# Feed-forward opening: normed tokens of the second half kept in fp32 by the norm, in place of sums of their two fp16 halves

## The chip, the cores and the metric

The kernel runs on one core of a Trainium2 chip. The metric is the device time of one execution in microseconds. The core has a matrix engine (TensorE, PE in the profile), three engines for elementwise work (VectorE is DVE, ScalarE is ACT, GpSimd is POOL) and DMA queues that are started here by SyncE (SP). Each engine works through its own instructions in order; semaphores hold an instruction until others have ended.

## The reference

Two layers of a transformer for 1024 latent and 256 context tokens of width 1024, everything in fp32. A layer is

```python
h  = rms_norm(x, norm_mix) * (1 + sc1) + sh1     # sc, sh, g: from the conditioning c
q, k, v, mlstm, gates, pool = split(h @ w_in)
x  = x + g1 * (concat(attention, mlstm, pool_mix) @ w_out)
h2 = rms_norm(x, norm_ffn) * (1 + sc2) + sh2
x  = x + g2 * ((silu(h2 @ w_gate) * (h2 @ w_up)) @ w_down)     # width 2816
```

The change lies between `h2` and the first products of the feed-forward. In the second layer the context tokens have no feed-forward.

## The kernel before

**Precision.** A product in fp32 is made of fp16 products: a value is split into a high half (its rounding to fp16) and a low half (the rest), and three matmuls (high by high, high by low, low by high) are summed. The usual split is one instruction of ScalarE for the high half and one of VectorE for the low half. Everything on chip lies as 128 partitions by columns; a token tile `h2[:, k, half, tokens]` holds feature block k of eight, its high or low half, and the tokens as columns. `h2` lies in the large tile T1 (`T_72` in the orders below), the queries, keys and values of the attention, and later the activations, in a second one, T2 (`T_73`). Rows of the profile call both `T`.

**The feed-forward** multiplies by blocks with seven products in place of eight, as Strassen did: the tokens are halved into H0 (0 to 511) and H1 (512 to 1023), the features into blocks 0 to 3 and 4 to 7. Three of the seven products need transformed tokens: with r11 = features 0-3 of H0, r12 = features 0-3 of H1 and r22 = features 4-7 of H1, T1 = r12 - r11, T3 = r22 - r12, T2 = r22 - T1. A fourth, T4, is (features 4-7 of H0) - T2. T1 to T3 are kept as split halves in tiles called `tq`; T4 is formed in fp32 in a part of T2 (`scv`) and written over H1 of `h2` when the plain H1 is no longer read. The weights are halved and summed in the same manner: their sums (`ws`) are made by GpSimd from raw tiles (`st`, `raw`) that SyncE fetches, and their split pieces (`hlp`) by ScalarE (high) and VectorE (low). Pieces are A11 to A22 and S1 to S4. The products (L1960) go to the banks Swa, Swb and Swc, a tile of weights with 512 tokens at a time; the sums and what follows are taken from the banks by VectorE.

**The norm** (`norm_k`, L595) makes `h2` from the residual X, for one feature block and some tokens: VectorE scales (`t<-X,prm,sq`, in fp32), ScalarE adds the shift and rounds (`T<-t,prm`, high half), VectorE makes the low half (`T<-t,prm,T`). Where the flag `mix` is set (blocks 2 and 5) ScalarE writes the shifted fp32 value back to `t`, then the high half, and GpSimd makes the low half. The tokens of H1 are normed in two parts of 256 columns: 512 to 767 while the output projection of the last part is still running (`wod`, splits of its weights `hlr`), and 768 to 1023 after it.

**The opening** (up to L1796) is the stretch between the norm and the seven-product steps. Ahead of it two strips of 128 gate and up features are multiplied plainly: `Sg`, `Su`, from which ScalarE makes Silu (`sg<-Sg`) and VectorE the gate product (`sg<-Su,sg`). While this runs, `h_ops` (L1544) is stepped four times, once per feature block k. A step rebuilds fp32 tokens as the sum of their halves (`rb<-T`, three), subtracts (`rb<-rb`, three), splits T3, T2 and T1 (three on ScalarE, three on VectorE: `tq<-rb,tq`) and updates T4 (`T<-T,rb`): ten instructions of VectorE. From the first gate product on VectorE keeps the order in which the program is written (`in_row(True)`); the other engines are ordered by a scheduler. The steps stand in that order by `next(ho)`: one ahead of the second `sg`, one behind it, in layer 0 one ahead of the last `sg` (768 columns), the rest behind the first weight pieces (`prepare()`).

**Buffers.** `t`, `rb`, `ws` and the squares share one ring of six buffers of 128x512 fp32, so each new tile waits until the one six places ahead of it has had its last reader. The raw weights have two `st` buffers, and the transfer into one is queued when its last reader is through. ScalarE also carries out the table loads ahead of a change of function.

Of the kernel before, what the change touches and what calls it, by code (L numbers as in the profile page):

```python
# [18 lines left out]
P = 128  # L19
# [62 lines left out]
def hybrid_kernel(ctx: ExitStack, tc: tile.TileContext, I, out, dbg=None):  # L82
# [89 lines left out]
    def act(o, i, f=AF.Copy, **kw):  # L172
        if f in (AF.Exp, AF.Ln) and tabs["kind"] != "el":
            preload()
        b = S.activation(o, i, f, **kw).ins  # L175
        if tabs.get("copy") is not None:
            tc.add_manual_dep(b, tabs["copy"].name, order, reason="behind the last copy")
        if f in (AF.Exp, AF.Ln):
            after(b, tabs["pre"])
            tabs["last"] = tabs["last"][-7:] + [b]  # L180
        elif f in (AF.Tanh, AF.Silu):
            if tabs["kind"] != f:
                for j in tabs["last"]:
                    after(b, j)
                tabs.update(last=[], kind=f)
            for j in tabs["last"][-1:]:
                after(b, j)
            tabs["last"] = [b]
        return b
# [397 lines left out]
    def rms_spread(s, ms, rr):  # L587
# [4 lines left out]
        act(r[:, :s.n], ms[:, :s.n])  # L592
        return r

    def norm_k(l, q, h, t0, n, k, r, pool=False, mix=False):  # L595
        s = 1 if t0 >= T else 0
        t = f2k((P, 512), F32, "t")
        stt(t[:, :n], X[:, k, t0:t0 + n], prm[l][:, q + 1, k, s:s + 1], r[:, :n], MUL, MUL)
        if pool:
            G.tensor_scalar(t[:, :n], t[:, :n], prm[l][:, q, k, s:s + 1], 1.0, op0=ADD, op1=MUL)  # L600
            act(h[:, k, 0, t0:t0 + n], t[:, :n])
            tt(h[:, k, 1, t0:t0 + n], t[:, :n], h[:, k, 0, t0:t0 + n], SUB, G)
            return
        if mix:
            act(t[:, :n], t[:, :n], AF.Identity, bias=prm[l][:, q, k, s:s + 1])
            act(h[:, k, 0, t0:t0 + n], t[:, :n])
            tt(h[:, k, 1, t0:t0 + n], t[:, :n], h[:, k, 0, t0:t0 + n], SUB, G)
            return
        act(h[:, k, 0, t0:t0 + n], t[:, :n], AF.Identity, bias=prm[l][:, q, k, s:s + 1])
        stt(h[:, k, 1, t0:t0 + n], t[:, :n], prm[l][:, q, k, s:s + 1], h[:, k, 0, t0:t0 + n], ADD, SUB)  # L610

    def norm(l, q, h, t0, n, sums, wait=1):
        for _ in range(wait):
# [153 lines left out]
    for l in range(DEPTH):  # L767
# [776 lines left out]
        def h_ops():  # L1544

            sl = [pt_((P, 2, 2, 512), F16, "phl", PHB, "tq") for _ in range(PHB)]
            sl += [pt_((P, 2, 2, 512), F16, "pT", PTB, "tq") for _ in range(6 - PHB)]
            pcs = [s[:, i] for s in sl for i in range(2)]
            for z, op in enumerate(("T1", "T2", "T3")):
                tpc[op] = pcs[4 * z:4 * z + 4]  # L1550
            for k in range(4):
                r12, r11, r22 = (f2k((P, 512), F32, "rb") for _ in range(3))
                for r, kk, c in ((r22, 4 + k, H1), (r12, k, H1), (r11, k, H0)):
                    tt(r, h2[:, kk, 0, c], h2[:, kk, 1, c], ADD)
                tt(r11, r12, r11, SUB)
                tt(r12, r22, r12, SUB)
                tt(r22, r22, r11, SUB)
                for op, r in (("T3", r12), ("T2", r22), ("T1", r11)):
                    split2(tpc[op][k], r, V)
                tt(scv[:, k], scv[:, k], r22, SUB)  # L1560
                yield
# [220 lines left out]
                fm(S_[:, t0:t0 + n], w, h2, t0, n)  # L1782
        wt = w = S_ = None
        act(sg[:, 512:NTq], Sg[:, 512:NTq], AF.Silu, scale=INV)
        if not last:
            next(ho)
        stt(sg[:, 512:NTq], Su[:, 512:NTq], 1.0 / SW, sg[:, 512:NTq], MUL, MUL)
        del Sg, Su
        hlt += [wk.tile([P, 2048], F16, tag="hl", name="hlp", bufs=2) for _ in range(2)]
# [278 lines left out]
```

## Time and profile before

| | |
|---|---|
| median of 3 runs | 2776.61 us (2774.57, 2776.61, 2776.82) |
| the profiled execution | 2780.47 us, its span 2778.7 us |
| instructions | 53623 |
| TensorE busy | 2564.7 us, 92% of the span, 21403 matmuls |
| VectorE busy | 1890.2 us, 68%, 3233 instructions |
| ScalarE busy | 1387.1 us, 50%, 2650 instructions |
| GpSimd busy | 1269.3 us, 46%, 963 instructions |
| granted TensorE clock, mean | 0.969 of 2.4 GHz |

The shares are means over the whole span, in which TensorE is the busiest by far. The change lies in two stretches of some 50 us, one in each layer (about 725 to 775 and 2145 to 2196 us), and in the norms ahead of them. What bounds the kernel there is read from the busy time of each engine in these stretches and from what TensorE waits for in them, not from the table.

### The profile page before, as it was taken

What the parts mean: (1) busy time and instruction counts of PE and PEld (TensorE: products, weight loads), DVE (VectorE), ACT (ScalarE), POOL (GpSimd) and SP (SyncE); (2) the same over time, 40 slices, a digit from 0 to 9 for tenths busy, and PEclk for the clock granted to TensorE, in tenths of its full rate; (3) what the DMA queues carried; (4) which work ended last, traced back from release to release, by engine and by line L of the source; (5) the groups of instructions that cost most, each with busy time, mean ns of one, the idle gap of its engine ahead of it and who ended that gap; (6) DMA issues with size and microseconds to landing.
All of it is one profiled execution on the core that took longest, in us unless ns stands there. A gap on an engine that the chain in (4) does not pass through costs nothing. (4 is left out here: it accounts for less than half of the span.)

```text
span 2778.7 us, 53623 instructions
## 1 busy us (share of the span) xinstructions
PE 2564.7 (92%) x21403; PEld 1500.9 (54%) x21403; DVE 1890.2 (68%) x3233; ACT 1387.1 (50%) x2650; POOL 1269.3 (46%) x963
## 2 busy tenths in 40 slices
PE   7999989987899999999999998888878899999997
PEld 4875556655555555555554684455545344444444
DVE  5558867778766555656565557866777767667676
ACT  5345557766443434444344544466765444444453
POOL 1124446774334435444443213456763465555651
PEclk9999999999899999999999999999989899999999
DMA  9544489995132222223212222389993111111211
GB/s 301 144 123 113 126 203 184 190 177 121 57 92 81 87 84 84 86 82 92 61 46 78 69 55 57 115 185 182 191 174 102 46 53 54 62 61 54 61 53 76
DMA packets 631629, 296.21 MB, mean 107 GB/s; under 512 B 362888, under 2 KB 620756, under 8 KB 630868
## 3 DMA queue, kind: packets, MB, share of 16 engines
q1 hardware_dynamic: 631204, 292.73, 42.9%
q8 instruction: 167, 2.74, 0.4%
q14 instruction: 82, 0.67, 0.1%
q10 hardware_dynamic: 176, 0.07, 0.0%
HBM read 176.19 MB, written 20.87 MB: 71 GB/s over the span
## 5 line engine op out<-in xcount | busy, mean ns | idle before, releaser
L1960 PEld LDWEIGHTS <-hlp 128*128 128x128 f16 x5040 | 492.0, 98 | 602.7 <-issue 26.6
L1960 PE MATMUL Swb<-T,hlp 128*128 128x512 f16 x1920 | 445.6, 381 | 18.5 <-DVE sg L96 13.0
L195 POOL TENSOR_TENSOR phl<-pf,phl 128x1280 f16<-128x1280 f32 (+1 forms) x132 | 345.2, 2618 | 176.8 <-ACT phl L175 123.1
L96 DVE SCALAR_TENSOR_TENSOR hlp<-ws,hlp 128x512 f16<-128x512 f32 (+1 forms) x320 | 231.6, 732 | 112.0 <-ACT hlp L175 89.2
L175 ACT ACTIVATE hlp<-ws 128x512 f16<-128x512 f32 (+1 forms) x320 | 162.6, 518 | 210.7 <-PE Swb L1960 90.5
L175 ACT ACTIVATE pf<-Sp,mx,rq 128x1280 f32<-128x1280 f32 (+1 forms) x144 | 189.6, 1317 | 118.1 <-DVE mx L96 98.8
L96 DVE TENSOR_REDUCE mx<-Sp 128x1 f32<-128x1280 f32 (+1 forms) x132 | 195.0, 1477 | 63.4 <-PE Sp L1337 55.4
L1960 PE MATMUL Swb<-tq,hlp 128*128 128x512 f16 x960 | 223.4, 382 | 8.0 <-DVE hlp L96 4.6
L1960 PE MATMUL Swc<-T,hlp 128*128 128x512 f16 x960 | 227.2, 379 | 0.0
L1400 PE MATMUL pwo<-T,hl 128*128 128x512 f16 (+1 forms) x960 | 194.5, 354 | 34.0 <-DVE X L96 14.3
L492 PE MATMUL pfm<-T,hl 128*128 128x512 f16 (+1 forms) x1032 | 216.4, 363 | 4.2 <-ACT E L175 4.1
L1337 PE MATMUL Sp<-T 128*128 128x512 f16 (+1 forms) x800 | 169.3, 348 | 42.5 <-ACT pf L175 40.1
L96 DVE SCALAR_TENSOR_TENSOR hlp<-st,hlp 128x256 f16<-128x256 f32 (+1 forms) x201 | 149.0, 746 | 86.7 <-ACT hlp L175 73.8
L195 POOL TENSOR_TENSOR ws<-st 128x256 f32<-128x256 f32 (+1 forms) x97 | 104.4, 1083 | 170.1 <-DMA st<-in_w_ffn_down_dram 67.9
L175 ACT ACTIVATE T<-sg 128x512 f16<-128x512 f32 (+1 forms) x170 | 98.8, 599 | 165.0 <-POOL sg L195 96.3
L1972 PE MATMUL dx<-T,hlp 128*128 128x256 f16 x1440 | 177.3, 273 | 1.0 <-DVE hlp L96 1.0
L195 POOL TENSOR_TENSOR X<-X,T 128x512 f32<-128x512 f32 x80 | 114.1, 1427 | 139.8 <-DVE X L96 105.1
L1960 PE MATMUL Swa<-T,hlp 128*128 128x512 f16 x720 | 169.3, 380 | 0.0
L1972 PEld LDWEIGHTS <-hlp 128*128 128x128 f16 x1440 | 139.1, 100 | 33.1 <-issue 4.8
L1400 PEld LDWEIGHTS <-hl 128*128 128x128 f16 x960 | 97.7, 102 | 109.8 <-issue 40.8
L175 ACT ACTIVATE phl<-pf 128x1280 f16<-128x1280 f32 (+1 forms) x115 | 144.6, 1262 | 21.2 <-DMA pT<-phl 18.9
L195 POOL TENSOR_TENSOR sg<-sg,T 128x512 f32<-128x512 f32 x60 | 88.7, 1478 | 143.6 <-DVE T L96 143.2
(308 smaller groups left out, 4735.8 us busy)
## 6 DMA issues: line engine op xcount, KB each, us to landing
T<-in_w_ada_dram SPq DMA_DIRECT2D x48, 512.0 KB
rawa<-in_w_ada_dram SPq DMA_DIRECT2D x48, 512.0 KB
st<-in_w_in_dram SPq DMA_DIRECT2D x32, 512.0 KB
st<-in_w_out_dram SPq DMA_DIRECT2D x64, 256.0 KB
st<-in_w_ffn_gate_dram SPq DMA_DIRECT2D x32, 512.0 KB
st<-in_w_ffn_up_dram SPq DMA_DIRECT2D x30, 512.0 KB
st<-in_w_ffn_down_dram SPq DMA_DIRECT2D x30, 512.0 KB
xs<-X SPq DMA_DIRECT2D x4, 2048.0 KB
```

Source lines behind the costliest of these rows:

```text
L96: b = f(*a, **k)
L175: b = S.activation(o, i, f, **kw).ins
L195: (e or V).tensor_tensor(o, a, b, op=op)
L492: mm(o, w[:, a, k, :], h[:, k, b, t0:t0 + n], start=(k == 0 and j == 0), stop=(k == nk - 1 and j == 2))
L1337: mm(Sp[:, e * nk + b0:e * nk + b0 + m], ql, qkv[:, 4 + h // 4, a, k0 + b0:k0 + b0 + m], start=(a == 0), stop=(a == 1), skip_group_check=True)
L1400: mm(pb, w[:, a, k, :], mixT[:, k0 + k, b, t0:t0 + n], start=(k == 0 and j == 0), stop=(k == 3 and j == 2))
L1960: mm(o, w[:, a, k, :], B[:, b], start=(s in "172" and k == 0 and j == 0), stop=(k == kh(i) - 1 and j == 2), skip_group_check=True)
L1972: mm(dbank[i][:, r * 256:(r + 1) * 256], w[:, a, k, :], B[:, b], start=(first and k == 0 and j == 0), stop=(not first and k == kh(i) - 1 a ...
```

## The change

The norm of the tokens 512 to 1023 ahead of the feed-forward also keeps its result in fp32. The place is a view `kept(k)` of T2, where the queries of the attention stood. For six of the eight feature blocks this is one more instruction of ScalarE, a copy of 128x256 with the shift added, behind the low half; for the two `mix` blocks the value is written there in place of `t`, with no further instruction. `h_ops` uses `kept(k)` and `kept(4 + k)` as r12 and r22, in place: two of its three adds go, and two of its three tiles of the ring. Over two layers and two norms each these are 24 copies, and 16 adds removed. Last, the step of `h_ops` ahead of the last `sg` in layer 0 goes; it is then made with the rest behind the weight pieces.

```diff
--- before.py
+++ after.py
@@ -592,6 +592,11 @@
         act(r[:, :s.n], ms[:, :s.n])
         return r
 
+    def kept(k):
+
+        j = 2 * (k % 4) + k // 4
+        return T2[:, j // 2, j % 2, 0:1024].bitcast(F32)
+
     def norm_k(l, q, h, t0, n, k, r, pool=False, mix=False):
         s = 1 if t0 >= T else 0
         t = f2k((P, 512), F32, "t")
@@ -601,13 +606,17 @@
             act(h[:, k, 0, t0:t0 + n], t[:, :n])
             tt(h[:, k, 1, t0:t0 + n], t[:, :n], h[:, k, 0, t0:t0 + n], SUB, G)
             return
+        keep = kept(k)[:, t0 - 512:t0 - 512 + n] if q and 512 <= t0 < T else None
         if mix:
-            act(t[:, :n], t[:, :n], AF.Identity, bias=prm[l][:, q, k, s:s + 1])
-            act(h[:, k, 0, t0:t0 + n], t[:, :n])
-            tt(h[:, k, 1, t0:t0 + n], t[:, :n], h[:, k, 0, t0:t0 + n], SUB, G)
+            v = t[:, :n] if keep is None else keep
+            act(v, t[:, :n], AF.Identity, bias=prm[l][:, q, k, s:s + 1])
+            act(h[:, k, 0, t0:t0 + n], v)
+            tt(h[:, k, 1, t0:t0 + n], v, h[:, k, 0, t0:t0 + n], SUB, G)
             return
         act(h[:, k, 0, t0:t0 + n], t[:, :n], AF.Identity, bias=prm[l][:, q, k, s:s + 1])
         stt(h[:, k, 1, t0:t0 + n], t[:, :n], prm[l][:, q, k, s:s + 1], h[:, k, 0, t0:t0 + n], ADD, SUB)
+        if keep is not None:
+            act(keep, t[:, :n], AF.Identity, bias=prm[l][:, q, k, s:s + 1])
 
     def norm(l, q, h, t0, n, sums, wait=1):
         for _ in range(wait):
@@ -1549,9 +1558,8 @@
             for z, op in enumerate(("T1", "T2", "T3")):
                 tpc[op] = pcs[4 * z:4 * z + 4]
             for k in range(4):
-                r12, r11, r22 = (f2k((P, 512), F32, "rb") for _ in range(3))
-                for r, kk, c in ((r22, 4 + k, H1), (r12, k, H1), (r11, k, H0)):
-                    tt(r, h2[:, kk, 0, c], h2[:, kk, 1, c], ADD)
+                r12, r22, r11 = kept(k), kept(4 + k), f2k((P, 512), F32, "rb")
+                tt(r11, h2[:, k, 0, H0], h2[:, k, 1, H0], ADD)
                 tt(r11, r12, r11, SUB)
                 tt(r12, r22, r12, SUB)
                 tt(r22, r22, r11, SUB)
@@ -1782,8 +1790,6 @@
                 fm(S_[:, t0:t0 + n], w, h2, t0, n)
         wt = w = S_ = None
         act(sg[:, 512:NTq], Sg[:, 512:NTq], AF.Silu, scale=INV)
-        if not last:
-            next(ho)
         stt(sg[:, 512:NTq], Su[:, 512:NTq], 1.0 / SW, sg[:, 512:NTq], MUL, MUL)
         del Sg, Su
         hlt += [wk.tile([P, 2048], F16, tag="hl", name="hlp", bufs=2) for _ in range(2)]
```

The first place is VectorE in the opening of layer 0, the rows up to the last gate product (`sg`, 768 columns). Before:

```order
L96 TENSOR_TENSOR tq<-rb,tq 128x512 [waits Activation_49] x2
L96 TENSOR_TENSOR tq<-rb,tq 128x512
L96 TENSOR_TENSOR T_73<-T_73,rb 128x512
L96 TENSOR_TENSOR rb<-T_72 128x512 x3
L96 TENSOR_TENSOR T_72<-T_73,T_72 128x512 [waits Activation_49]
L96 TENSOR_TENSOR rb<-rb 128x512 [waits DVE_49]
L96 TENSOR_TENSOR T_72<-T_73,T_72 128x512 [waits Activation_49]
L96 TENSOR_TENSOR rb<-rb 128x512 [waits DVE_49] x2
L96 TENSOR_TENSOR tq<-rb,tq 128x512 [waits Activation_49] x2
L96 TENSOR_TENSOR tq<-rb,tq 128x512
L96 TENSOR_TENSOR T_73<-T_73,rb 128x512
L96 SCALAR_TENSOR_TENSOR sg<-Su,sg 128x768 [waits PE_49]
```

And with the change, from the second gate product on:

```order
L96 SCALAR_TENSOR_TENSOR sg<-Su_10590,sg 128x512 [waits PE_49]
L96 TENSOR_TENSOR rb<-T_72 128x512
L96 TENSOR_TENSOR sg<-sg 128x512 [waits Pool_49]
L96 TENSOR_TENSOR rb<-T_73,rb 128x512 [waits DVE_49]
L96 TENSOR_TENSOR T_73<-T_73 128x512 [waits DVE_49]
L96 TENSOR_TENSOR T_73<-T_73,rb 128x512 [waits DVE_49]
L96 TENSOR_TENSOR tq<-T_73,tq 128x512 [waits Activation_49] x2
L96 TENSOR_TENSOR tq<-rb,tq 128x512
L96 TENSOR_TENSOR T_73<-T_73 128x512
L96 TENSOR_TENSOR T_73<-sg,T_73 128x512 [waits DVE_49,Activation_49]
L96 TENSOR_TENSOR T_72<-T_73,T_72 128x512 [waits Activation_49] x2
L96 SCALAR_TENSOR_TENSOR sg<-Su,sg 128x768 [waits PE_49]
```

The three sums `rb<-T_72` of a step became one, the differences are written into T_73 itself, and the last `sg` stands ten instructions further ahead, behind the second step and not the third.

The second place is ScalarE at the end of the norm of tokens 768 to 1023 in layer 0, up to the first Silu. Before:

```order
L175 ACTIVATE T_72<-t,prm_141 128x256 [waits DVE_49] x2
L175 ACTIVATE t<-t,prm_141 128x256 [waits DVE_49]
L175 ACTIVATE T_72<-t 128x256 [waits Activation_49]
L175 ACTIVATE T_72<-t,prm_141 128x256 [waits DVE_49] x2
L175 ACT_TABLE_LOAD
L175 ACTIVATE sg<-Sg 128x1280 [waits PE_49]
```

And with the change:

```order
L175 ACTIVATE T_72<-T_73 128x256 [waits Activation_49]
L175 ACTIVATE T_73<-t,prm_141 128x256
L175 ACTIVATE T_72<-t,prm_141 128x256 [waits DVE_49]
L175 ACTIVATE T_73<-t,prm_141 128x256
L175 ACTIVATE T_73<-t,prm_141 128x256 [waits DVE_49]
L175 ACTIVATE T_72<-t,prm_141 128x256 [waits DVE_49]
L175 ACTIVATE T_72<-T_73 128x256 [waits Activation_49]
L175 ACTIVATE T_73<-t,prm_141 128x256
L175 ACTIVATE T_72<-t,prm_141 128x256 [waits DVE_49]
L175 ACTIVATE T_73<-t,prm_141 128x256
L175 ACT_TABLE_LOAD
L175 ACTIVATE sg<-Sg 128x1280 [waits PE_49]
```

Between the high halves (`T_72<-t,prm`) now stand the copies (`T_73<-t,prm`), two of them directly ahead of a row that VectorE releases, one ahead of the table load for the Silu.

The third place is GpSimd in the opening of layer 1: the sums of weights (`ws`) of the first pieces. Before:

```order
L195 TENSOR_TENSOR ws<-st 128x512 [waits DMAHW5_49,Pool_49]
L195 TENSOR_TENSOR T_73<-sg,T_73 128x512 [waits Activation_49]
L195 TENSOR_TENSOR ws<-ws,st 128x512 [waits DVE_49,Activation_49,Pool_49]
L195 TENSOR_TENSOR ws<-st,ws 128x512 [waits DVE_49,Activation_49,Pool_49]
L195 TENSOR_TENSOR ws<-raw 128x512 [waits DMAHW6_49,DVE_49,Pool_49]
```

And with the change:

```order
L195 TENSOR_TENSOR ws<-st 128x512 [waits DMAHW5_49]
L195 TENSOR_TENSOR T_73<-sg,T_73 128x512 [waits Activation_49] x2
L195 TENSOR_TENSOR ws<-ws,st 128x512 [waits Pool_49]
L195 TENSOR_TENSOR ws<-st,ws 128x512 [waits PE_49,Pool_49]
L195 TENSOR_TENSOR ws<-raw 128x512 [waits DMAHW6_49,DVE_49]
```

The order of the sums is the same, but where a sum waited for VectorE and ScalarE to be through with a buffer of the ring it now waits for TensorE or for nothing of theirs.

## Rows read from the trace of the kernel before

**Rows 1.** Busy time by stretch, layers 0 and 1; columns in row one.

```profile
core 0: us, PE busy (x) PEld busy (x) DVE busy (x) ACT busy (x) POOL busy (x), PEclk, DMA share, GB/s
724.80:773.28 48.48, 38.55 (x221) 20.49 (x219) 46.46 (x61) 21.46 (x39) 14.80 (x10) 0.89 0.11 33
2145.40:2195.60 50.20, 38.34 (x149) 15.40 (x147) 45.59 (x61) 20.77 (x37) 17.01 (x11) 0.83 0.07 22
747.40:756.40 9.00, 0.03 (x1) 0.00 (x0) 8.93 (x13) 3.15 (x5) 1.91 (x2) 0.63 0.20 58
756.40:773.28 16.88, 15.92 (x91) 8.03 (x91) 16.88 (x25) 8.58 (x17) 4.36 (x3) 0.89 0.11 32
...
2167.70:2195.70 28.00, 20.01 (x64) 7.25 (x64) 24.07 (x34) 10.93 (x20) 10.81 (x7) 0.72 0.06 20
```

**Rows 2.** TensorE waits, 700-800, 2100-2230 us: total us, times, longest.

```profile
PE Swb L1960 <- DVE sg L96: 9.0, 1, 9.0
...
PE Swb L1960 <- DVE hlp L96: 4.6, 1, 4.6
...
PE Swb L1960 <- DVE sg L96: 4.0, 1, 4.0
PE Swb L1960 <- ACT hlp L175: 3.2, 2, 2.5
```

**Rows 3.** Timeline, VectorE, layer 0: start, us, instruction, [idle before].

```profile
724.81 1.49 DVE L96 SCALAR_TENSOR_TENSOR sg<-Su,sg 128x1280 f32<-128x1280 f32 x1 [2.06 <-ACT sg L175]
726.22 1.89 DVE L96 TENSOR_TENSOR rb<-T 128x512 f32<-128x512 f16 x3
729.78 0.69 DVE L96 TENSOR_TENSOR sg<-sg 128x512 f32<-128x512 f32 x1 [1.68 <-POOL T L195]
...
744.73 4.03 DVE L96 TENSOR_TENSOR rb<-T 128x512 f32<-128x512 f16 x3
...
755.47 0.94 DVE L96 SCALAR_TENSOR_TENSOR sg<-Su,sg 128x768 f32<-128x768 f32 x1
...
772.69 0.68 DVE L96 SCALAR_TENSOR_TENSOR hlp<-st,hlp 128x512 f16<-128x512 f32 x1
```

**Rows 4.** Groups by form, VectorE, 724.7-773.4 us: busy us, mean ns.

```profile
L96 DVE TENSOR_TENSOR rb<-T 128x512 f32<-128x512 f16 x12 | 11.7, 1030 | 0.0
```

**Rows 5.** Timeline, GpSimd, layer 0, 744-748 us.

```profile
744.34 1.60 POOL L195 TENSOR_TENSOR ws<-st 128x512 f32<-128x512 f32 x1 [0.68 <-POOL ws L195]
...
746.01 1.60 POOL L195 TENSOR_TENSOR ws<-ws,st 128x512 f32<-128x512 f32 x1
```

**Rows 6.** Timeline, ScalarE, layer 0, norm of tokens 768 to 1023.

```profile
716.52 0.91 ACT L175 ACTIVATE T<-t,prm 128x256 f16<-128x256 f32 x2 [0.55 <-DVE t L96]
...
721.72 0.51 ACT L175 ACTIVATE T<-t,prm 128x256 f16<-128x256 f32 x1 [0.32 <-DVE t L96]
...
723.54 1.24 ACT L175 ACTIVATE sg<-Sg 128x1280 f32<-128x1280 f32 x1
```

**Rows 7.** Timeline, ScalarE and TensorE, layer 0, last output projection.

```profile
692.85 0.62 ACT L175 ACTIVATE hlr<-st 128x512 f16<-128x512 f32 x1
...
705.80 1.06 ACT L175 ACTIVATE hlr<-st 128x1024 f16<-128x1024 f32 x1 [3.14 <-DMA st<-in_w_ffn_gate_dram]
...
709.60 1.01 PE L582 MATMUL ms<-ones,sq 128*128 128x1 f32 x4 [2.95 <-DVE sq L96]
```

**Rows 8.** Timeline, layer 1, the four engines, 2180 to 2199 us.

```profile
2180.49 1.56 POOL L195 TENSOR_TENSOR ws<-ws,st 128x512 f32<-128x512 f32 x1 [10.72 <-DVE tq L96]
...
2190.84 0.63 ACT L175 ACTIVATE hlp<-ws 128x512 f16<-128x512 f32 x1 [2.90 <-POOL ws L195]
...
2192.02 1.29 DVE L96 TENSOR_TENSOR tq<-rb,tq 128x512 f16<-128x512 f32 x2 [2.34 <-ACT tq L175]
...
2194.43 1.16 DVE L96 SCALAR_TENSOR_TENSOR hlp<-ws,hlp 128x512 f16<-128x512 f32 x1
...
2195.76 2.76 PE L1960 MATMUL Swb<-tq,hlp 128*128 128x512 f16 x12 [0.66 <-ACT hlp L175]
```

## The prediction

> **What bounds the kernel now.** I read the busy shares by stage first, then TensorE's waits in the two stages that the change touches, then VectorE's own sequence there, and last what ScalarE and GpSimd do beside it. Over the whole program TensorE is the bound. In the opening of each feed-forward it is not. From 724.80 to 773.28 us (layer 0) VectorE is busy 46.46 of 48.48 us with 61 instructions, and from 2145.40 to 2195.60 us (layer 1) 45.59 of 50.20 us, also with 61 [rows 1]. In the same stretches TensorE waits: 9.0 us in layer 0 for `sg`, the last gate product; 4.0 us for `sg`, 4.6 us for VectorE's `hlp` and 3.2 us for ScalarE's `hlp` in layer 1 [rows 2]. Its clock is below full speed around them: 0.89 of 2.4 GHz granted from 756.40 to 773.28, and 0.72 from 2167.70 to 2195.70, so part of it ran at the 1.2 GHz level [rows 1].
>
> So a microsecond of VectorE taken out ahead of the last row that TensorE needs is worth a microsecond, until something else is late. That last row is in layer 0 the low half of weight piece A21 (`hlp<-st`, 772.69), behind which TensorE runs on without long waits; in layer 1 it is the low half of piece S1 (2194.43 to 2195.6), after which TensorE starts 12 products at 2195.76 in 2.76 us, full speed [rows 3, 8].
>
> **The eight adds that go (per layer).** Of the 12 `rb<-T` adds that rebuild fp32 tokens from two fp16 halves, 8 are removed. Their mean is 1030 ns [rows 4], but three of them took 1.89 us from 726.22, where one alone is about 0.68: they follow each other at 0.60 us [rows 3]. The excess comes from GpSimd: the three from 744.73 took 4.03 us [rows 3] while GpSimd ran two `ws` sums of 1.60 us from 744.34 and 746.01 [rows 5], so 4.03 - 1.89 = 2.14 us, or 1.07 for each GpSimd instruction, were lost. The ten GpSimd instructions of this stretch [rows 1] are all still there and will stop whatever VectorE does instead. I therefore take 8 x 0.60 = 4.8 us a layer, and not 8 x 1.03 = 8.2; 9.6 for both, bound 16.5.
>
> The Trainium skill says the same of the cause (SBUF — State Buffer, "Who interferes with whom"): a VectorE instruction with two SBUF inputs and a GpSimd instruction that reads SBUF share a port, and the one that comes second is blocked for the whole of the other. The trace agrees with 1.07 us lost to 1.60 us of GpSimd. The rule speaks against counting the adds at their mean: by it the sum stays at 9.6, and only by the means would it be 16.5.
>
> **The order in layer 0.** The removed third step of the helper stood ahead of the last `sg` product, ten instructions of VectorE. Now `sg` (755.47 before) can run once its matmuls are done at 747.4 [rows 1, 3]. VectorE gets there in: start 726.7 (1.9 later than now, below), 1.4 for the first product (724.81 to 726.22 [rows 3]), 21 x 0.60 = 12.6, five GpSimd holds of 1.07, and 1.2 for ScalarE's halves, together 747.3. TensorE's wait of 9 us there shrinks to about 2. But the step stands behind it now, and the products T3 and T2 of token block 3 need it. TensorE reaches them after 48 products at up to 0.216 us (2.76 us less one end, by 12 [rows 8]), some 9 us later, at about 758, while VectorE still has 24 instructions and three or four holds, until about 767. The wait moves; it does not go. What counts is when VectorE comes to A21: 52 instructions in place of 61, 8 removed and one (`T<-T,T`) moved behind, 0.6 us more. TensorE also has three products less to do after it, 0.6 us.
>
> **Waits of VectorE that go.** In layer 0 the wait of 1.68 us for GpSimd before `sg<-sg` goes [rows 3], since that row now stands one add into the next step. In layer 1 a wait of 2.34 us goes: VectorE stood for ScalarE's half of `tq`, ScalarE for `ws` in order ahead of it (2.90), and GpSimd had waited 10.72 us for a buffer of the ring of six that `rb` held [rows 8]. With two of three `rb` tiles out of the ring, the row of GpSimd no longer waits for VectorE. Together 4.0 (bounds 0 and 4.0). New waits for ScalarE's halves, whose sources now come faster one after another, I take as 1.5 and 0.5, one such wait of 2.34 us [rows 8] at most in all (bounds 0 and 4).
>
> **What is added: the copies on ScalarE.** 24 copies of 128x256, six in each of four norms. One takes 0.51 us; two in a row took 0.91 [rows 6], so a queue of them goes at 0.40. In the norm of the last 256 tokens ScalarE now has 16 instructions, 16 x 0.40 = 6.5 us from 716.52, and ends at 723.0 where its last one before started at 721.72 and was through at 722.2: the Silu behind it, at 723.54, comes 0.8 us later [rows 6]. In the norm ahead of it the split of `hlr` at 692.85 stands behind those copies in ScalarE's order; the output weights' buffers, their next transfers, the gate weight (705.80) and at last the sum of squares for which TensorE waited 2.95 us at 709.60 follow from it [rows 7]. I pass 1.0 us on in layer 0 and 0.6 in layer 1, where the transfers start from VectorE's row and not from ScalarE's. Late start: 1.9 + 1.5 = 3.4 us. Bounds: 0, if the gaps hide all; 24 x 0.51 = 12.2, if nothing is hidden.
>
> **Clock.** TensorE's waits stay, so it comes out of them at the lower level once more. Before, the granted clock of 0.89 cost 0.11 x 16.88 = 1.9 us in layer 0 [rows 1], most of it hidden under VectorE. I charge 1.0 and 0.7 (bounds 0 and 3.8).
>
> **Sum.** 9.6 + 0.6 + 4.0 - 2.0 - 3.4 + 0.6 - 1.7 = 7.7 us gained, about 3.3 in layer 0 and 4.4 in layer 1. Against the profiled execution of 2780.5 us that is 2772.8; the median of the runs, 2776.6, lies 3.9 below that execution, and I give 2776.6 - 7.7 = 2768.9. A difference of 0.2% (5.55 us) is about what a measurement of this kernel can tell from no change.
>
> **Rivals.** (A) *The late start eats half.* Each of the twelve copies of a layer delays its norm by 0.35, between 0 and its 0.40 in a queue [rows 6], and the weights' transfers pass it on: a slip of 12 x 0.35 = 4.2 a layer in place of 1.7. For it: those splits stand directly behind the copies. Against: ScalarE is idle for part of both norms. 7.7 - 5.0 = 2.7, so 2773.9, within 0.2%. (B) *No slip, no new waits.* The copies fit into the gaps and VectorE runs at its pitch: 9.6 + 0.6 + 4.0 + 0.6 - 0.4 = 14.4, so 2762.2. For it: ScalarE's load in the openings is under half. Against: the norms themselves are its busiest places. (C) *Slower: ScalarE becomes the bound of the norms.* Place: the two norms of 256 tokens in each layer, ahead of the Silu. Price: nothing hidden, 12.2; the wait at 709.60 doubles and the lower clock lasts longer, 2 x 1.9 = 3.8; less the 9.6: 6.4 us slower, 2783.0. It decides once the first Silu comes over 4.8 us later in a layer, more than the eight adds give back. Against: that needs copies at 0.51 in a queue, and the row shows 0.40. (D) *The change does nothing*: the copies are written over the queries of the attention and could wait for its last reader, or the wait only moves and TensorE is late anyway: about 2776. Against the first half: no row of the new order waits for TensorE at a copy, and the adds are gone from VectorE's rows.
>
> **Chances.** Forecast (2764 to 2771) 0.50, B 0.10: faster 0.60. A 0.25, D 0.05: same 0.30. C: slower 0.10. The range runs from B's 2762 to D's 2776 and leaves out about 2 in 10.
>
> **What would show it.** Right: VectorE has 8 instructions less in each stretch and its `rb<-T` adds are four a layer; the Silu of 128x1280 comes 1 to 3 us later, counted from the end of the attention; TensorE's wait before the first transformed product is near 2 us in layer 0, with a new one of 3 to 6 us before the last tokens of T3; the stretches end 3 and 4 to 5 us earlier. Wrong: a Silu over 4 us late (A, C); GpSimd's sums falling into VectorE's last 24 rows in place of its idle time before `sg`; or TensorE, and not VectorE, late at A21 and S1.

## The result and the profile after

The changed kernel takes 2761.98 us (median of 5 runs, 2759.21 to 2765.98), the kernel before 2776.61 us in the same comparison (2774.57 to 2778.45). The ratio is 0.9948 with a 95% interval of 0.9934 to 0.9962: 14.6 us faster, between 10.6 and 18.3. The forecast was 7.7 us faster, 2768.9; the measured time lies at the lower end of its range (2762 to 2776), where rival B stood with 2762.2. The profiled execution of the change took 2761.98 us, its span is 2759.8.

TensorE still has the same 21403 matmuls, VectorE has 3217 instructions in place of 3233 and ScalarE 2674 in place of 2650: 16 adds less, 24 copies more. First the stretches from the first gate product to the low halves of A21 (layer 0) and S1 (layer 1), as in [rows 1]; then two stretches of TensorE's waiting within them. Columns: start and end, length, busy time of each engine with its instructions, granted clock, share and rate of DMA.

```profile
725.80:766.90 41.10, 37.41 (x214) 19.57 (x212) 40.64 (x53) 21.07 (x40) 19.31 (x10) 0.96 0.09 26
2134.60:2176.50 41.90, 34.49 (x143) 14.13 (x142) 40.53 (x54) 20.39 (x36) 24.44 (x10) 0.88 0.08 26
753.00:768.50 15.50, 12.53 (x79) 6.44 (x77) 15.49 (x27) 10.68 (x20) 7.91 (x2) 0.89 0.14 38
2153.70:2180.00 26.30, 19.90 (x75) 7.64 (x75) 25.25 (x33) 12.16 (x21) 21.72 (x8) 0.81 0.16 55
```

The 48.48 and 50.20 us of [rows 1] are 41.10 and 41.90 us now, 7.4 and 8.3 less, and VectorE is as full as before (40.64 of 41.10). TensorE's clock is a little better there, 0.96 and 0.88 for 0.89 and 0.83, but it still falls in places: 0.89 from 753.00 to 768.50 and 0.81 from 2153.70 to 2180.00, so part of each ran at the 1.2 GHz level. TensorE's waits in layer 0, 690 to 800 us (total us, times, longest):

```profile
PE pwod L1409 <- ACT hlr L175: 2.8, 3, 1.9
PE pada L515 <- ACT sa L175: 1.9, 1, 1.9
PE Sg L1450 <- POOL T L195: 1.7, 1, 1.7
PE Swb L1966 <- ACT T L175: 1.0, 1, 1.0
PE Swb L1966 <- DVE sg L96: 0.8, 1, 0.8
```

and in layer 1:

```profile
PE Swb L1966 <- ACT hlp L175: 3.1, 1, 3.1
PE Swc L1966 <- DVE tq L96: 2.4, 2, 1.8
PE Swb L1966 <- DVE sg L96: 1.8, 1, 1.8
```

The 9.0 us for `sg` in layer 0 [rows 2] are 0.8; in their place stand 1.9 us (`sa`, products of the conditioning that ScalarE copies out of a bank late) and 1.0 us (`T<-Swb`, with which ScalarE empties a bank). The lines `pwod` and `Sg` lie ahead of the opening. A wait for the last tokens of T3, which the prediction had put at 3 to 6 us, is not among them; in the second trace of the change it is 0.6 us. Gone too is what TensorE waited in the kernel before for the low half of A21:

```profile
PE dx L1972 <- DVE hlp L96: 1.0, 1, 1.0
```

In layer 1 the 4.6 us for VectorE's `hlp` are gone, the 4.0 for `sg` are 1.8, the 3.2 for ScalarE's `hlp` stayed at 3.1, and 2.4 for tokens (`tq`) are new. VectorE's own rows (timeline: start, us, instruction), in layer 0

```profile
725.85 1.49 DVE L96 SCALAR_TENSOR_TENSOR sg<-Su,sg 128x1280 f32<-128x1280 f32 x1 [3.22 <-ACT sg L175]
727.26 0.68 DVE L96 TENSOR_TENSOR rb<-T 128x512 f32<-128x512 f16 x1
...
734.19 1.16 DVE L96 TENSOR_TENSOR rb<-T 128x512 f32<-128x512 f16 x1
...
746.45 0.96 DVE L96 SCALAR_TENSOR_TENSOR sg<-Su,sg 128x768 f32<-128x768 f32 x1
...
766.22 0.68 DVE L96 SCALAR_TENSOR_TENSOR hlp<-st,hlp 128x512 f16<-128x512 f32 x1
```

and in layer 1:

```profile
2134.69 1.22 DVE L96 SCALAR_TENSOR_TENSOR sg<-Su,sg 128x1024 f32<-128x1024 f32 x1 [3.00 <-ACT sg L175]
...
2175.32 1.16 DVE L96 SCALAR_TENSOR_TENSOR hlp<-ws,hlp 128x512 f16<-128x512 f32 x1
```

The low half of A21 starts 40.4 us behind the first gate product, where it was 47.9 (724.81 to 772.69 [rows 3]); S1's 40.6 us behind its own, where it was 48.9 (to 2194.43 [rows 8] from this row of the kernel before):

```profile
2145.49 1.23 DVE L96 SCALAR_TENSOR_TENSOR sg<-Su,sg 128x1024 f32<-128x1024 f32 x1 [1.85 <-ACT sg L175]
```

Of three `rb<-T` in a row one is left.

### The profile page after: what moved, and what is told of

Its sections match the earlier page's. It is cut to its first block, busy times and chain, and to the rows that moved or that the text cites. A ratio compares the mean times of both kernels' runs of the same rounds, so it can differ in the third digit from the quotient of the medians.

```text
span 2759.8 us, 53616 instructions
## 1 busy us (share of the span) xinstructions
PE 2559.2 (93%) x21403; PEld 1500.7 (54%) x21403; DVE 1882.9 (68%) x3217; ACT 1393.8 (51%) x2674; POOL 1288.3 (47%) x963
## 5 line engine op out<-in xcount | busy, mean ns | idle before, releaser
L1346 PE MATMUL Sp<-T 128*128 128x512 f16 (+1 forms) x800 | 171.2, 351 | 43.1 <-ACT pf L175 40.9
```

What stands on the lines that cost most here:

```text
L1346: mm(Sp[:, e * nk + b0:e * nk + b0 + m], ql, qkv[:, 4 + h // 4, a, k0 + b0:k0 + b0 + m], start=(a == 0), stop=(a == 1), skip_group_check=True)
```

## Where the time went, stage by stage

Every trace has 21403 matmuls. Some of them stand in another order from kernel to kernel, but only within the norm and the opening, and the four numbers used here lie outside these places, so that each marks one place in every kernel (in late_t4b the order differs a little beyond number 7900). Two lengths are read in each layer: the **start**, from a matmul at the beginning of the norm of tokens 512 to 767 (number 7380, 18380) to the first gate product of VectorE, and the **path**, from that gate product to a matmul just behind the opening (number 7900, 18780; in the trace after it lies in the 24 `Swb` that start at 774.97). All in us.

| kernel | start, layer 0 | path, layer 0 | start, layer 1 | path, layer 1 |
|---|---|---|---|---|
| before | 37.85 | 58.75 | 29.56 | 59.78 |
| before, second trace | 34.04 | 58.73 | 29.90 | 58.78 |
| the change | 36.21 | 51.07 | 29.88 | 52.00 |
| the change, second trace | 37.01 | 50.77 | 30.70 | 53.19 |
| copies_only | 36.58 | 59.23 | 30.21 | 59.64 |
| no_copies | 33.77 | 53.02 | 31.80 | 54.38 |
| kept_only | 36.90 | 54.74 | 30.44 | 53.36 |
| order_only | 34.11 | 61.77 | 29.71 | 59.60 |
| ring_only | 34.28 | 57.69 | 31.99 | 58.71 |
| ring_order | 34.29 | 60.55 | 29.76 | 58.74 |
| copies_dve | 37.18 | 50.75 | 34.43 | 53.24 |
| copies_twice | 42.08 | 50.72 | 34.75 | 54.32 |
| late_t4b | 36.93 | 51.67 | 32.10 | 56.02 |

The paths are 7.8 us (layer 0) and 6.7 us (layer 1) shorter, by the means of two traces each. The starts are later: without copies layer 0 has 33.8 to 34.3 in five of six traces, and 36.2 to 37.0 with them, 2.6 us more; layer 1 has 29.6 to 29.9 in four and 29.9 to 30.7 with them (32.1 in late_t4b), 0.6 more by the change's two. That is 14.5 gained and 3.2 lost, 11.3 us, inside the interval of the measured 10.6 to 18.3 but below its middle. The other 3 us lie in no stage that the change touches. Between the feed-forward of layer 0 and the start in layer 1 (matmul 12400 to 18380, the attention for the most part), for instance, where TensorE's rows are the same, the two traces of before are 643.4 and 641.1 us long and the two of the change 638.9 and 636.5, and the other kernels, whatever their change, lie between 636.5 and 642.0. What of that is chance is not settled.

The 37.85 of the first trace stands alone. It is the norm of [rows 7], where TensorE waited 2.95 us for the sum of squares. In the second trace of the same kernel the same rows read:

```profile
705.59 0.61 PE L582 MATMUL ms<-ones,sq 128*128 128x1 f32 x4 [1.66 <-DVE sq L96]
706.05 1.14 PE L1441 MATMUL Su<-T,hl 128*128 128x256 f16 x9
707.03 1.24 PE L1441 MATMUL Sg<-T,hlr 128*128 128x512 f16 x5
708.11 0.61 PE L589 MATMUL ms<-idn,rr 128*128 128x128 f32 x4
```

The wait is 1.66 us, and the nine `Su` behind it take 1.14 us. In the first trace they took 2.08, and the four `ms<-ones` 1.01 for 0.61:

```profile
710.47 2.08 PE L1441 MATMUL Su<-T,hl 128*128 128x256 f16 x9
```

The granted clock was 0.50 from 709.60 to 712.60 us there, the 1.2 GHz level, and 1.00 from 705.59 to 708.50 in the second. So the wait of [rows 7] belonged to that one execution, and a part of the difference of the two profiled spans (2778.7 and 2759.8) has nothing to do with the change.

## Experiments

Two theories stood at the beginning. V: the gain is VectorE's rows ahead of A21 and S1, and the copies cost a little. N: part of it comes out of the norms, where TensorE's rows stand in another order with the copies. For layer 0 a third, O: what counts is the step that no longer stands ahead of the last gate product. Times are given as the difference to the kernel before, by the ratio of the runs with its interval.

**copies_only.** The steps are those of before, the norm that of the change.

```diff
             for k in range(4):
-                r12, r22, r11 = kept(k), kept(4 + k), f2k((P, 512), F32, "rb")
-                tt(r11, h2[:, k, 0, H0], h2[:, k, 1, H0], ADD)
+                r12, r11, r22 = (f2k((P, 512), F32, "rb") for _ in range(3))
+                for r, kk, c in ((r22, 4 + k, H1), (r12, k, H1), (r11, k, H0)):
+                    tt(r, h2[:, kk, 0, c], h2[:, kk, 1, c], ADD)
...
+        if not last:
+            next(ho)
```

> The 24 copies of the norm are made as in the change, but nothing reads them: the three sums of each step, their order and their buffers are those of before. Theory V (the gain is VectorE's: rows and waits taken out between the first gate product and the pieces A21 and S1; copies only cost): the last norm of each layer is 1.4 us longer, as it is in the profile after, so 2.8 us slower than before, 2779.4. Rival N (part of the gain comes out of the norms: with the copies TensorE's rows there stand in another order, its wait for the sum of squares shrank from 2.95 to 0.69 us and its clock stayed up): layer 0 starts 1.6 us earlier, layer 1 0.3 later, so 1.3 us faster than before, 2775.3.

Measured: 2.5 us slower (0 to 5.0), near the 2.8 of V; N's gain lies outside the interval. The price is in the starts, +2.5 in layer 0 and +0.5 in layer 1; the paths are 0.4 to 0.5 longer.

**no_copies.** The steps are those of the change, made from the high halves alone.

```diff
-                r12, r22, r11 = kept(k), kept(4 + k), f2k((P, 512), F32, "rb")
-                tt(r11, h2[:, k, 0, H0], h2[:, k, 1, H0], ADD)
-                tt(r11, r12, r11, SUB)
-                tt(r12, r22, r12, SUB)
-                tt(r22, r22, r11, SUB)
+                r12, r22, r11 = kept(k), kept(4 + k), f2k((P, 512), F32, "rb")
+                h12, h22 = h2[:, k, 0, H1], h2[:, 4 + k, 0, H1]
+                tt(r11, h2[:, k, 0, H0], h2[:, k, 1, H0], ADD)
+                tt(r11, h12, r11, SUB)
+                tt(r12, h22, h12, SUB)
+                tt(r22, h22, r11, SUB)
```

> The norm is that of before, without copies; the steps take only the high halves of the tokens of the second half in place of the kept fp32 (the low halves are left out of T1 to T4 there), write into the same places of T2, and the third step stands behind the last gate product as in the change. So VectorE's rows in the opening are those of the change, and ScalarE's in the norm those of before. Theory V: the change without the cost of its copies, 14.6 + 2.8 = 17.4 us faster than before, 2759.2. Rival N: the gain of the norms is missing, 14.6 - 1.3 = 13.3 us faster, 2763.3, and TensorE waits near 3 us for the sum of squares in layer 0 again, at the lower clock.

Measured: 8.3 us faster (5.0 to 11.7). Both theories missed: without its copies the change is not faster. The start of layer 0 is 2.8 us earlier than with them, but the path from there is 2.1 us longer (53.02 for 50.9). TensorE waits 0.8 us for the last `sg` in both: its own plain products ahead of that end the race, and what VectorE wins at the start it waits for there (2.01 us idle ahead of that `sg`, none with the change). So in layer 0 most of the price of the copies lies in time that is not missed. The path of layer 1 is 1.8 us longer too, for another reason: VectorE's rows lose 1.6 us more beside GpSimd and come to S1 42.2 us behind the first gate product (40.6 with the change). (In layer 1 the start of this run and that of ring_only hold a stretch at the lower clock: the 21 `Su` behind the sum of squares took 4.12 us, at a granted clock of 0.57 and 0.58, where they took 2.45 at 1.00 in the traces of the kernel before.)

**kept_only and order_only.** The change without its removed step, and before with only the step removed.

```diff
         act(sg[:, 512:NTq], Sg[:, 512:NTq], AF.Silu, scale=INV)
+        if not last:
+            next(ho)
         stt(sg[:, 512:NTq], Su[:, 512:NTq], 1.0 / SW, sg[:, 512:NTq], MUL, MUL)
```

> The change, but in layer 0 the third step stands ahead of the last gate product again, as before. Theory V: TensorE's wait for the last gate product comes back with 4 to 6 us, but the piece A21, eight rows of VectorE later in any case, comes at the same time within 1 us: 0 to 2 us slower than the change, 2762 to 2764. Rival O (in layer 0 the gain is the removed step ahead of the gate product): the wait is lost in full, 5 to 6 us slower than the change, 2767 to 2768.

> The kernel before, with only the third step ahead of the last gate product in layer 0 moved behind it. Theory V: TensorE starts its first transformed-weight product some 6 us earlier, waits there for the tokens instead, and A21 comes one row of VectorE (0.6 us) and at most the one wait of 1.7 us earlier: 0.5 to 2 us faster than before, 2774.5 to 2776. Rival O: 5 us faster or more, 2771 or less.

Measured: kept_only 8.9 us faster than before (5.6 to 12.2), its path in layer 0 3.8 us longer than the change's. The path lies between V and O, the time, 5.7 us behind the change, at O. order_only 3.3 us slower than before (-0.3 to 6.9), its path in layer 0 3.0 longer; against both. The two parts need each other: in layer 0 the kept tokens alone shorten the path by 4.0 us, the order alone lengthens it by 3.0, both together shorten it by 7.8. In kept_only TensorE has one wait of the opening,

```profile
PE Swb L1968 <- DVE sg L96: 7.8, 1, 7.8
```

and none behind it: with the adds gone, TensorE's own products from that gate product on are the bound, not VectorE's way to A21. Only then does an earlier gate product pay. In order_only TensorE starts earlier and is stopped later. The chain in the timeline of all engines:

```profile
762.38 1.88 DVE L96 TENSOR_TENSOR rb<-T 128x512 f32<-128x512 f16 x3
...
762.59 5.21 POOL L195 TENSOR_TENSOR ws<-raw 128x512 f32<-128x512 f32 x1 [9.11 <-issue]
...
767.20 1.15 DVE L96 TENSOR_TENSOR rb<-rb 128x512 f32<-128x512 f32 x1
767.83 0.63 ACT L175 ACTIVATE hlp<-ws 128x512 f16<-128x512 f32 x1 [4.54 <-POOL ws L195]
...
768.52 0.90 PE L1958 MATMUL Swc<-tq,hlp 128*128 128x512 f16 x2 [4.55 <-ACT hlp L175]
```

VectorE runs row after row without a break from 755.76 to 768.35; GpSimd's sum `ws<-raw`, 1.60 us in the kernel before, takes 5.21 us; ScalarE's split `hlp<-ws` waits 4.54 us for it and TensorE 4.55 us for the split.

**ring_only and ring_order.** Before, with two of three sums of a step written to the places in T2 (all adds stay); the second also with the step moved.

```diff
-                r12, r11, r22 = (f2k((P, 512), F32, "rb") for _ in range(3))
+                r12, r22, r11 = kept(k), kept(4 + k), f2k((P, 512), F32, "rb")
```

> The kernel before, with two of the three sums of a step written to the places in T2 that the change uses, in place of tiles of the ring: all adds stay, no copies, the order of before; only the ring is relieved. Theory V (the gain is the eight adds a layer; the ring matters in one place): the stretch from the 24 matmuls of the first Su to the end of the opening stays at 51.9 us within 1 in layer 0, and in layer 1 loses GpSimd's wait of 10.7 us for a buffer and with it VectorE's wait of 2.3, so 49.3 becomes 46 to 47; 2 to 3 us faster than before. Rival R (the ring is what held the opening): layer 1 as with the change, 42.5 to 44, and layer 0 at least 2 us shorter, so 7 to 8 us faster.

> All adds stay and no copies are made, but two of three sums of a step lie in T2 and not in the ring, and in layer 0 the third step stands behind the last gate product, as in the change. Alone, the relieved ring made the opening of layer 0 1.1 us shorter (50.8 of 51.9) and the order 3.0 longer (54.9). Theory V: without the removed adds VectorE is still the bound and comes to A21 no earlier than with the order alone: 53 to 55 us. Rival P (the order loses because a sum of GpSimd waits for a tile of the ring that the moved step holds; the two parts need each other): with the ring relieved the order gains, 48 to 50 us.

Measured: ring_only 3.3 us faster (0.8 to 5.8) with paths 1.0 and 0.6 shorter; ring_order the same as before (-2.8 to 2.2), its path in layer 0 1.8 longer. GpSimd's wait of 10.72 us in layer 1 [rows 8] is gone, as the prediction said; a wait for a half of ScalarE's stands ahead of that place now. The columns are start, us, instruction, idle time before it:

```profile
2163.03 5.69 POOL L195 TENSOR_TENSOR T<-sg,T 128x512 f16<-128x512 f32 x1 [7.74 <-ACT T L175]
2168.68 1.27 POOL L195 TENSOR_TENSOR ws<-ws,st 128x512 f32<-128x512 f32 x1
2170.03 1.60 POOL L195 TENSOR_TENSOR ws<-st,ws 128x512 f32<-128x512 f32 x1
```

but the path gains only 0.6 of it: GpSimd now stands 5.69 us in one split beside VectorE's adds. And with the moved step TensorE waits as in order_only:

```profile
PE Swc L1963 <- ACT hlp L175: 5.3, 1, 5.3
```

So the ring is not what makes the order lose (P falls). That it is VectorE's adds follows from what is left: with eight of them gone too, the same order gains. By the paths the relieved ring alone is worth 1.6 of 14.5 us, a tenth of the gain; by the time, 3.3 us.

**copies_dve and copies_twice.** The copies on VectorE; and each made twice on ScalarE.

```diff
         if keep is not None:
-            act(keep, t[:, :n], AF.Identity, bias=prm[l][:, q, k, s:s + 1])
+            V.tensor_scalar(keep, t[:, :n], prm[l][:, q, k, s:s + 1], 1.0, op0=ADD, op1=MUL)
...
+            act(keep, t[:, :n], AF.Identity, bias=prm[l][:, q, k, s:s + 1])
             act(keep, t[:, :n], AF.Identity, bias=prm[l][:, q, k, s:s + 1])
```

> The change with its 24 copies on VectorE (a sum of one tile and a column of scalars) in place of ScalarE. If ScalarE's queue in the last norm is what makes the first Silu late (1.4 us a layer in the profile after), it comes that much earlier: 2 to 3 us faster than the change, about 2759. Rival: VectorE is as busy there; six more instructions of 0.3 to 0.4 us make its own queue 2 us longer: 1 to 3 us slower than the change, 2763 to 2765.

> The change with each of the 24 copies made twice into the same place. If the copies lie in gaps of ScalarE (the norm of layer 0 took 41.2 to 42.0 us with them and 40.6 to 41.1 without), a second set is partly hidden too: the norms 1 to 2 us longer a layer, 2 to 4 us slower than the change. Rival (ScalarE is the bound of the norm with the first set already): six more rows of 0.40 in each norm of 256 tokens, 2.4 us for the last and up to 2.4 for the one ahead of it, 5 to 10 us slower.

Measured: copies_dve 13.3 us faster than before (10.0 to 16.7), with the change's 14.6 inside; the starts are 37.18 and 34.43, not earlier. In the total the two engines cannot be told apart. In layer 1 they can: there the start is 4.1 us later than with the change, and TensorE waits 3.6 us for ScalarE's splits `hlr` where it waits 0.3. copies_twice is 5.0 us faster than before (2.5 to 7.2), so it gives back 9.6 of the change's 14.6; that is the rival's 5 to 10. ScalarE in the norm of tokens 768 to 1023:

```profile
716.98 2.90 ACT L175 ACTIVATE T<-t,prm 128x256 f16<-128x256 f32 x7 [0.55 <-DVE t L96]
...
723.19 2.63 ACT L175 ACTIVATE T<-t,prm 128x256 f16<-128x256 f32 x6
...
727.13 1.73 ACT L175 ACTIVATE sg<-Sg 128x1280 f32<-128x1280 f32 x2
```

The change's own rows there (with [rows 6] for before):

```profile
716.21 2.50 ACT L175 ACTIVATE T<-t,prm 128x256 f16<-128x256 f32 x6 [0.55 <-DVE t L96]
...
721.22 1.29 ACT L175 ACTIVATE T<-t,prm 128x256 f32<-128x256 f32 x3
...
724.58 1.73 ACT L175 ACTIVATE sg<-Sg 128x1280 f32<-128x1280 f32 x2 [0.77 <-PE Sg L1450]
```

22 instructions from 716.98 to 725.84 without a gap, 0.40 each, where the change has 16 from 716.21 to 722.53 and before had 10. The first set of copies costs 3.2 us in the two starts together, 0.13 for one; the second 9.9 (42.08 and 34.75 for 36.6 and 30.3), 0.41 for one, its length in a queue: the gaps of ScalarE were used up by the first.

**b2 and a2.** The two kernels once more, for second traces.

> The kernel before again, for a second trace. Theory V': the 2.95 us for which TensorE waited for the sum of squares in layer 0, and the low clock behind it, belong to that one execution: two kernels with the same norm waited 1.6 and 1.7 us at full clock. Then the stretch from the norm of tokens 512 to 767 to the end of the 24 matmuls of Su (44.7 us in the first trace) is 40 to 42 us, and the opening behind it 51 to 53 us as in the first. Rival N (that norm is slow by its order, and the change mends it): 44 to 45 us again.

> The change again, for a second trace. Theory V: the stretch from the 24 matmuls of the first Su to the end of the opening is 46 us in layer 0 and 42 to 44 in layer 1, as in the first trace and the other kernels with the same rows of VectorE there; the norm ahead of it in layer 0 is 41 to 42 us. Rival N: the norm varies by less than 0.5 us from trace to trace.

The norm stage that the expectation names came out as 40.9 us where it was 44.7, and 42.0 with the change (41.2 in the first trace). N falls: the norm is not mended by the change, and the first trace of before was the exception. With the change it is 0.7 us longer in the mean, no more than its two traces differ. a2 was 16.7 us faster than before (11.7 to 21.7).

**late_t4 and late_t4b.** If VectorE's rows ahead of A21 are the bound, seven fewer of them should pay as the eight adds did. T4's updates were moved behind the weight pieces, made from the two halves of T2.

```diff
                     split2(tpc[op][k], r, V)
-                tt(scv[:, k], scv[:, k], r22, SUB)
...
-            stt(o[:, 1], src, SW, o[:, 0], MUL, SUB)
+            b = V.scalar_tensor_tensor(o[:, 1], src, SW, o[:, 0], op0=MUL, op1=SUB)
             made[i, p] = o
+            if (i, p) == (0, "A22" if has_ctx else "S1"):
+                for k in range(4):
+                    for a in range(2):
+                        d = V.tensor_tensor(t4[:, k], t4[:, k], tpc["T2"][k][:, a], op=SUB)
+                        tc.add_manual_dep(d.ins, b.ins.name, order, reason="behind A22, S1")
+                    split2(h2[:, k, :, H1], t4[:, k], V)
```

> The change, with the four updates of T4 and its low halves taken out of VectorE's rows ahead of A21 and S1: T4 is made from the two halves of T2 (eight rows in place of four) behind the piece S1. If VectorE's rows ahead of A21 and S1 are what bounds the opening still, seven rows of 0.60 us less in layer 0 and four to seven in layer 1 make it 2.5 to 4 us shorter in each (46 to 42-43.5, 43 to 39-40.5): 5 to 7 us faster than the change, 2755 to 2757. Rival: TensorE is the bound there by now, or the eight later rows make the next weight pieces late: 0 to 2 us faster, 2760 to 2762.

> The change, with T4 made from the halves of T2 (eight updates in place of four) behind the piece A22 in layer 0 and S1 in layer 1, as in the run before, but in a place of T2 of its own: there TensorE's results were copied out into the very tile that the late updates still used, and TensorE waited 2.6 us for that. In layer 0 that run was 4.9 us ahead of the change when the piece A21 was through, and gave it back. If VectorE's rows ahead of A21 and S1 bound the opening, the openings are now 42 to 44 us in layer 0 (46 with the change) and 39.5 to 42 in layer 1 (42.5 to 43.7): 3 to 7 us faster than the change. Rival: TensorE's products, ScalarE's splits and GpSimd's starved sums are the bound by now: 45 to 46 and 42 to 44 us, within 2 us of the change.

In late_t4 the updates share their tile with TensorE's results that are copied out meanwhile, so its T4 is not that of the reference; it was 3.3 us faster than before (0.3 to 6.1), and only the start of its opening is read. late_t4b was 7.2 us faster than before (4.2 to 10.6), some 7 us behind the change; both expectations missed, and the rival, within 2 us of the change, was too kind. In layer 0 VectorE (late_t4b) reaches A21 (761.29) 37.4 us behind the first gate product, 3 us sooner than with the change (2 of the 4.9 us named above were there before the opening began). Then

```profile
761.29 0.68 DVE L96 SCALAR_TENSOR_TENSOR hlp<-st,hlp 128x512 f16<-128x512 f32 x1
...
764.90 3.09 DVE L96 TENSOR_TENSOR T<-T,tq 128x512 f32<-128x512 f32 x5
767.91 1.28 DVE L96 TENSOR_TENSOR T<-T,T 128x512 f16<-128x512 f32 x2
...
773.07 1.75 DVE L96 SCALAR_TENSOR_TENSOR hlp<-raw,hlp 128x512 f16<-128x512 f32 x1
...
776.42 1.75 DVE L96 TENSOR_TENSOR T<-T,T 128x512 f16<-128x512 f32 x1
```

the late rows stand ahead of the next weight piece (`hlp<-raw`, 773.07), and from 771.40 on VectorE's rows are stretched to 1.75 us beside four sums of GpSimd in a row. TensorE waits 2.4 us for that piece:

```profile
PE Swb L1970 <- DVE hlp L96: 2.4, 1, 2.4
PE Swc L1970 <- ACT tq L175: 2.3, 1, 2.3
```

(The 2.3 us for `tq` lie ahead of A21.) The path in layer 0 is not shorter than with the change, and in layer 1, where the late rows stand behind S1, it is 3.4 us longer. Rows that are moved behind A21 or S1 come back as the next wait; the eight adds paid because they are gone.

## Why the prediction was right, and where its sizes were off

**What bounds.** Right in layer 1, and by a narrow margin in layer 0: VectorE stayed full through the opening, but TensorE, 9.0 us late from the last `sg`, had only 1.0 us to wait for A21 in the kernel before. no_copies shortens the paths by 5.7 and 4.9 us without a copy, copies_only by nothing.

**The eight adds at 0.60 us.** Right. Nine rows less on the way to A21 are 5.4 of the 7.5 us by which that way shrank in layer 0, eight rows 4.8 of 8.3 in layer 1. GpSimd's holds did not go with the adds: a row of VectorE that meets one is still about 1.07 us longer, and all rows of layer 0 together are 9.6 us longer than 0.60 each where they were 10.1 (the wide `sg` rows included). At their mean of 1030 ns the adds would have been worth 16.5 us, more than the paths gave. The Trainium skill (SBUF — State Buffer, "Who interferes with whom") has the one that comes second blocked for the whole of the other instruction. The trace agrees for VectorE; GpSimd lost more than one instruction of VectorE's (last section). That the 9.6 us of holds stayed is what kept the price of the adds at 0.60.

**Waits of VectorE.** The 1.68 us before `sg<-sg` are gone as said. In layer 1 VectorE waited 4.4 us in all and 1.1 after, so 3.3 were won for the 2.3 named. But the 2.0 us charged for new waits on ScalarE's halves did not come: 0.2 us in layer 0. This is the first term that was mis-sized, with the one before some 3 us too small together.

**The order in layer 0.** The wait for `sg` was forecast near 2 us and is 0.8, the new one for the last tokens of T3 3 to 6 and is 0 and 0.6 in the two traces; TensorE stood 1.9 us just ahead of them and 1.0 behind, for ScalarE's copies out of banks. What failed is the sentence that the wait moves and does not go, and that only 0.6 us for one row and 0.6 for TensorE hang on it: kept_only shows 3.8 us. The prediction took VectorE's arrival at A21 as the bound in every case; with the adds gone, TensorE's products behind `sg` are as late, so both ends had to move, and both did.

**The copies.** 3.4 us of late start were charged, 1.9 and 1.5; 2.6 and 0.6 were measured at the first gate product. The term was right in sum, and in layer 0 so was its way: TensorE waits 2.8 us for `hlr` there, and 0.7 to 1.3 in the kernels without copies. The Silu is not held by ScalarE's queue alone: it stands 0.77 us for `Sg` (724.58), whose products waited 1.7 us for GpSimd's low half of a `mix` block, 0.8 in every trace without copies. That this price hardly reaches the end in layer 0 (no_copies) the prediction did not see. The 2.95 us of [rows 7], from which it argued in part, belonged to that one execution. ScalarE in a queue goes at 0.40 us, as read from [rows 6]: 22 rows in 8.86 us.

**Clock.** 1.7 us were charged; the clock of the stretches rose instead, from 0.89 to 0.96 and from 0.83 to 0.88, with shorter waits of TensorE in both.

**The sum.** For the paths 5.2 and 5.9 were forecast and 7.8 and 6.7 measured; for the starts 3.4 in all were forecast and 3.2 measured. That makes 11.3 in place of 7.7. The median says 14.6; the 3 us between are not found in the stages of the change, and with the time at the very end of the range, on which side of that end it fell is luck. Rival B came nearest by its number, 14.4, though its condition, no slip, did not hold: the slip came, and the paths gained more. A (copies pass nearly their full length on) falls for the first set and is what copies_twice shows for a second; C (slower) needed the copies at 0.51 in a queue, and they took 0.40; D falls with the result.

## What to carry to other kernels

Cost a removed instruction at its pitch on a free engine and not at its mean beside a neighbour that stops it: the neighbour stops the next one instead. Before work is given to another engine, count the gaps in that engine's queue there; the first set of copies went into them at 0.13 us each, the second at 0.41. And where two paths are nearly equal (an engine's rows to one point, another's products from an earlier one), a change to either alone pays little or loses; undo each part by itself to see it.

## What the runs showed of the hardware

The block between VectorE and GpSimd is lopsided. VectorE loses about 1.07 us to one GpSimd instruction, but GpSimd beside a run of VectorE's two-input instructions loses far more: sums and splits of 1.2 to 1.7 us took 5.21 (order_only) and 5.69 us (ring_only), and in layer 1 of the change

```profile
2158.80 1.26 POOL L195 TENSOR_TENSOR ws<-ws,st 128x512 f32<-128x512 f32 x1
...
2161.70 1.72 POOL L195 TENSOR_TENSOR ws<-raw 128x512 f32<-128x512 f32 x1
2167.11 8.83 POOL L195 TENSOR_TENSOR ws<-raw,st 128x512 f32<-128x512 f32 x1 [3.69 <-DVE tq L96]
2176.01 1.59 POOL L195 TENSOR_TENSOR ws<-ws,raw 128x512 f32<-128x512 f32 x1
```

a sum took 8.83 us, from 2167.11 to 2175.94, all the time in which VectorE ran two-input rows back to back. In late_t4 a split of half the size took longer still:

```profile
756.39 3.61 POOL L195 TENSOR_TENSOR T<-sg,T 128x256 f16<-128x256 f32 x1 [6.50 <-ACT T L175]
761.80 10.24 POOL L195 TENSOR_TENSOR T<-sg,T 128x256 f16<-128x256 f32 x1 [1.80 <-ACT T L175]
772.00 1.71 POOL L195 TENSOR_TENSOR ws<-raw,st 128x512 f32<-128x512 f32 x1
```

GpSimd's spans are rough in a profile, but the split of ScalarE and the products of TensorE behind it (767.83 and 768.52 in order_only) start when such a span ends. Each of the spans ends 0.6 to 1.2 us after VectorE comes to a row that takes one input from a bank (`sg<-Swa,T` at 766.60 in order_only and 2174.72 in the change, `prm<-pada` at 771.43 in late_t4) or stands still (2167.70 in ring_only).

The second is the chance in the clock. The same 21 `Su` of layer 1's norm took 2.45 us at a granted clock of 1.00 behind a wait of 1.33 us in the kernel before, and 4.12 us at 0.57 and 0.58 behind waits of 1.54 and 1.56 us in no_copies and ring_only, with the same order of rows; in ring_order they took 2.45 us behind 1.55. And the first trace of before has such a stretch in layer 0: 3.8 us in one start, half of what was forecast for the change. A stage of one trace is a sample; here the second trace of the same kernel settled what its order of rows could not.
